# One tile pool for the up and down products, and five scan chunks moved from the output projection into the second half of the input projection

## The chip, the cores and the metric

The kernel runs on one core of one Trainium2 chip. The core has five engines that run their own instruction streams and meet through semaphores: TensorE (PE, matrix products into PSUM), VectorE (DVE), ScalarE (ACT), GpSimd (POOL) and SyncE (SP), whose queue (SPq) issues all DMAs of this kernel. The metric is the time of one execution on the device, in microseconds. Three runs of the kernel before took 2654.14, 2654.44 and 2649.2 us, a median of 2654.14.

## The reference

One layer of a sequence model on x of 2048 frames by 1024 channels, all in float32:

```python
h = rmsnorm(x, norm_mix_w)
u_b, u_c, u_h, z, xbc, dt_raw = split(h @ w_in)          # 3 x 1024, 1024, 1536, 16 columns
y_a = u_b * causal_conv3(u_c * u_h)                       # short convolution mixer
y_b = ssd_mixer(z, xbc, dt_raw, ...)                      # conv4 + SiLU on x/B/C, state scan, gate, grouped norm
x = x + concat(y_a, y_b) @ w_out
h = rmsnorm(x, norm_mlp_w)
x = x + square(relu(h @ w_up)) @ w_down                   # 1024 -> 4096 -> 1024
return rmsnorm(x, final_norm_w)
```

The mixer `ssd_mixer` has 16 heads in 2 groups. Its scan runs over chunks of the sequence: in a chunk, `y = (C B^T * decay) (x dt) + C state * exp(a)`, and then the state is decayed and gets the chunk's own `B^T (x dt decay_end)`. The reference writes chunks of 64 frames; the kernel takes 128 (`L`), which gives the same result, so there are 2 groups x 16 = 32 (group, chunk) units, in the list `CHUNKS` (line 1179), ordered by block of 512 frames, then group, then chunk. Units 0 to 15 belong to the first 1024 frames, 16 to 31 to the second.

## The kernel before

**Products.** Each float32 factor is split into a rounded part `hi` and a rest `lo` (ACT casts, line 100 or 205; DVE subtracts, line 101 or 206), and one product is three matmuls: hi hi, hi lo, lo hi. The large products (input projection, up, down) use a scheme of seven block products in place of eight: a 2 x 2 block product from sums and differences of blocks, in `Seven.chain` (line 245). Its seven products run in the order `b11, t1, t2, b21, t3, b22, t4`, each 12 matmuls of 128 x 128 by 128 x 512 when four pieces of the inner dimension are summed, so 84 for a *pair* of column tiles. After each product, `evict` takes a sum out of PSUM, `ahead` prepares weights of the next pair, and the callback `after(name)` interleaves other work.

**Stages,** in the order of time: the first half of the input projection (frames 0 to 1023), the second half (frames 1024 to 2047), the output projection in 64 units of 24 matmuls, up (two halves of 16 pairs), down with the final norm.

**The second half** (`second_half`, line 815) runs the 22 pairs of the list `LATER`; a name is the kind and the first tile: z (gate), x (inputs of the scan; x8 and x10 are B and C), ch (C and h of the short convolution), b. An x pair ends with two convolutions over 1024 frames (`conv`, line 679): one ACT pass, three DVE passes (line 685), a SiLU, a store to `xs_d`; one starts behind `b22`, one behind `t4`. Beside the pairs runs `side`, the generator `scan.run` (line 1330): `after` takes one step of it behind each of the seven products. It covers chunks 0 to 15.

**The scan.** With one set of buffers (`bufs` = 1, in the second half) a chunk takes 9 steps: `back` 1 (TensorE: `st`, `yo`, `yd`; DVE updates the state and adds), `back` 2 (adds D x from the tile `xd`, multiplies by the gate `y`) together with the loads of the next chunk (`bc`, `xd`, `dec`, `eb`), `back` 3 (squares), an empty step, `front` 1 of the next chunk (TensorE transposes x into `ptx` and B into `ptb`), `back` 4 (`pss`, the norm), `front` 2, `back` 5 (stores to `yn_d`) with the load of the next gate, `front` 3. In `front` (line 1245), step 2 has ACT do the decays (8 passes of line 1268, an exponential, line 1269), four multiplications by D (1271) and the cast `hi` of the weighted x (1276); step 3 has DVE subtract `lo` (1278) and multiply the decays by the masked scores (1279). `st` needs `hi` and `lo`, `yd` needs the decays. The tiles `xd`, `dec` and `y` have one buffer in the second half and two in the output projection, where a chunk takes 8 steps.

**The output projection.** A hook runs twice in each unit, behind 12 matmuls; in units 0 to 47 hook `at` takes `1 + at % 2` steps of the scan, for chunks 16 to 31. At hooks fixed by `schedule` (line 1498) blocks of y are fetched and split by ACT and DVE (`fill`, lines 1425 to 1427). From unit 48 on no scan runs.

**Up and down.** The pool `up` has eight tiles `utmp` of 512 columns, five `uhid` of 2 x 512 and two `facc`. A pair of up fills three `uhid` (e0, e1, e2), squares the relu on ACT, takes four differences on DVE (`sums`) and stores seven blocks to `hid_d` with four DMAs. When the stage ends, that pool closes and `down` (line 981) opens the pool `dp` in the same memory: 18 accumulators `acc`. `outs` (973) loads four of them for each d from x1; `evict` (line 1018) adds the sums of the down product into them. The steps of down (`STEPS`, line 1164) are: d = 0 with four inner tiles, d = 2 with two, then d = 1 with one and d = 3 with three together.

**Order on the engines.** A pool's slots go round: a new tile waits for the last reader of the tile that had its slot. The framework lays out each engine's instructions with some freedom: where one must wait, a later one that is ready may be placed ahead of it. On the chip each engine then keeps that order. Four PSUM banks take the sums of up and down (`x`, `y`), two more the sums `w`.

Of the kernel before, what the change touches and what calls it, by code (L numbers as in the profile page):

```python
# [39 lines left out]
def trunk(ctx: ExitStack, tc: tile.TileContext, x, w_in, w_dt, w_out, w_up, w_down, cvec, hrow, out):  # L40
# [150 lines left out]
    class Seven:  # L191
# [18 lines left out]

        def sums(self, e0, e1, e2, t4):

            self.sub(e2[:, 0], e2[:, 1], e0[:, 1])
            self.sub(e0[:, 1], e0[:, 1], e0[:, 0])
            self.sub(e1[:, 0], e2[:, 1], e0[:, 1])
            self.sub(t4, e1[:, 1], e1[:, 0])
# [210 lines left out]
    class Proj(Seven):  # L427
# [5 lines left out]
        LATER = "z0 x0 z4 ch0 ch1 b0 x8 ch2 ch3 b2 x2 ch4 ch5 b4 x4 x10 ch6 ch7 b6 x6 z6 z2".split()  # L433
# [381 lines left out]
        def second_half(self, ws, side):  # L815

            self.dt_weights()
            dts = itertools.chain(*(self.dt_part(NBB + bb) for bb in range(NBB)))
            for m, what in enumerate(self.LATER):
                last = m + 1 == len(self.LATER)  # L820
                ahead = self.plain(w_out[0], (0, 1)) if last else self.weights(1, self.LATER[m + 1])

                def after(name):
                    if m or name == "t4":
                        next(dts, None)
                    next(side, None)
                    if last:
                        proj_out.enter(self, name)

                ws = self.pair(1, what, ws, ahead, after)  # L830
            return ws

    class Mlp(Seven):
# [18 lines left out]
        def wide(self, name):  # L852
            return self.up.tile([P, 2, TB], F32, tag="uhid", name=name, bufs=5)

        def store(self, h, q, e0, e1, e2):
            t4 = self.tmp("t4")
            if h == 1 and q >= LAST:
                nc.sync.dma_start(b12_d[:, q - LAST], e0[:, 1])
            self.sums(e0, e1, e2, t4)
            for i, e in enumerate((e0, e1, e2)):  # L860
                nc.sync.dma_start(hid_d[h][q][:, 2 * i : 2 * i + 2], e)
            nc.sync.dma_start(hid_d[h][q][:, 6], t4)

        def pair(self, h, q, ws, ahead, after):

            e0, e1, e2 = (self.wide(n) for n in ("e0", "e1", "e2"))
            s = {}
# [5 lines left out]
            def add(o, pm, name):  # L873
                nc.vector.tensor_tensor(out=o, in0=pm, in1=s[name], op=ALU.add)
# [5 lines left out]
            def evict(name, gi, pm):  # L880
# [3 lines left out]
                elif name == "t1":  # L884
                    copy(pm["y"], "s5")
                elif name == "t2":
                    copy(pm["x"], "s2")
                elif name == "b21":
                    if gi in self.seeds:
                        relu2(e0[:, 0], pm["w"])  # L890
                    else:
                        add(e0[:, 0], pm["w"], "s1")
                        relu2(e0[:, 0], e0[:, 0])
                elif name == "t3":
                    add(e2[:, 1], pm["x"], "s5")
                    relu2(e2[:, 1], e2[:, 1])
                elif name == "b22":
                    add(e0[:, 1], pm["y"], "s2")
                    relu2(e0[:, 1], e0[:, 1])
                else:  # L900
                    relu2(e1[:, 1], pm["x"])

            got = self.chain([self.places], ws, ahead, evict, after)
            self.store(h, q, e0, e1, e2)
# [152 lines left out]
        def rest(self, ws):  # L1057
# [11 lines left out]
            sums = [self.dp.tile([P, TB], F32, tag="acc", name="facc", bufs=18) for _ in range(NBB)]  # L1069
# [34 lines left out]
        def norm_out(self, tiles, bb, ts, st, *sums):  # L1104
# [3 lines left out]
            r = st.spread()  # L1108
# [14 lines left out]
        def rstd(self, w=TB):  # L1123
            return Rstd(self.dp, lambda n: self.raw(n)[:, 0], D, w)

        def finish_first(self):

            for bb in range(NBB):
# [8 lines left out]
                acc = self.dp.tile([P, TB], F32, tag="facc", name="facc", bufs=1)  # L1137
# [41 lines left out]
    CHUNKS = [(b, g, c) for b in range(NB) for g in range(G) for c in range(NC)]  # L1179

    class Scan:
# [63 lines left out]
        def front(self, n):  # L1245
# [19 lines left out]

            dec = t["dec"]
            for i in range(HG):
                nc.scalar.activation(dec[:, i], dec[:, i], AF.Relu, bias=t["a"][:, i : i + 1], scale=-1.0)  # L1268
            nc.scalar.activation(dec, dec, AF.Exp, scale=-1.0)
            for j in range(4):  # L1270
                nc.scalar.mul(t["xd"][:, j], t["xd"][:, j], col(C_D, 4 * g + j))
            for k, by in (("xdt", "dt"), ("xde", "dend")):
                t[k] = self.tmp()
                nc.vector.tensor_tensor(out=byhead(t[k]), in0=byhead(xtok), in1=t[by], op=ALU.mult)
            hi, lo = t["parts"] = [a.bitcast(F32R) for a in (self.tile([512], "xtok", 1), self.tmp())]
            nc.scalar.copy(hi, t["xde"])
            yield
            nc.vector.tensor_tensor(out=lo, in0=t["xde"], in1=hi.bitcast(F32), op=ALU.subtract)
# [241 lines left out]
    with ExitStack() as c1:  # L1520
# [68 lines left out]
    mlp.down(c4, ws)  # L1589
# [57 lines left out]
```

## Time and profile before

| what | value |
|---|---|
| three runs | 2654.14, 2654.44, 2649.2 us; median 2654.14 |
| the profiled execution | 2651.32 us, of which the span of its instructions is 2649.1 us |
| mean granted TensorE clock | 0.995 |
| TensorE busy | 2597.8 us, 98% of the span |
| VectorE busy | 1926.7 us, 73% |
| ScalarE busy | 1455.0 us, 55% |
| DMA | 536.96 MB, 203 GB/s over the span |

The busy time of TensorE counts a matmul from its start to the end of its pipeline, 390 ns for one of 512 columns, though the next starts 227 ns later; so idle time counts, and not the share of busy time. A table of windows gives busy time by engine in a stretch of time; a list of waits names the engine that waited, what it waited for, the sum, how often, and the longest; a timeline has one row for each instruction, or for a run of like ones, with its start, its length, and in brackets the idle time ahead of it and what ended that.

### The profile page before, as it was taken

The numbers are of one execution on the slowest core, as the hardware profiler recorded it, in microseconds if no ns is written. First come the engines' busy times: TensorE is split into PE (matmuls) and PEld (weight loads), VectorE is DVE, ScalarE is ACT, GpSimd is POOL, SyncE is SP. The second block draws the span as 40 slices with busy tenths as digits, with TensorE's granted clock in tenths as the row PEclk, the third lists the DMA queues.
The fourth block names the chain that finished last, engine by engine and source line by source line (L and its number), as shares of the span: only waits on it lengthen the run. The fifth ranks groups of instructions, "written<-read, shape, count | busy, mean of one in ns | idle before, by whom it ended". The sixth has DMA issues, their size and how long they took to land.

```text
span 2649.1 us, 33645 instructions
## 1 busy us (share of the span) xinstructions
PE 2597.8 (98%) x12056; PEld 2133.7 (81%) x12056; DVE 1926.7 (73%) x2652; ACT 1455.0 (55%) x2212; POOL 54.0 (2%) x98
## 2 busy tenths in 40 slices
PE   7999999999999999999999999999999999999998
PEld 5788888788878888877888888888887888888887
DVE  7977867777778767767677775744447877888885
ACT  6654345776667666857336555755555444444543
POOL 0010000000000000000000000000000000000001
PEclk9999999999999999999999999999999999999999
DMA  3545745555555588877656786765558544665762
GB/s 145 197 175 187 274 143 200 185 161 171 175 163 165 163 272 258 265 205 220 202 203 230 258 314 238 273 216 192 197 194 290 155 151 150 217 205 176 244 207 69
DMA packets 292871, 536.96 MB, mean 203 GB/s; under 512 B 26208, under 2 KB 141920, under 8 KB 292704
## 3 DMA queue, kind: packets, MB, share of 16 engines
q1 hardware_dynamic: 292704, 534.82, 61.4%
q8 instruction: 94, 1.54, 0.2%
q14 instruction: 73, 0.60, 0.1%
HBM read 354.89 MB, written 179.83 MB: 202 GB/s over the span
## 4 chain that ended last, share of the span: by engine, by line
PE 61%; issue 25%; DMA 6%; ACT 5%; DVE 2%; SPq 0%; POOL 0%; POOLq 0%; DVEq 0%; ACTq 0%
PE px L276 9%; PE px L277 9%; PE px L278 9%; PE py L276 4%; PE py L278 4%; PE py L277 4%; PE pm L113 3%; PE pm L114 3%; PE pm L115 3%; DMA dec<-rd_d 3%; PE pw L276 2%; PE pw L278 2%; PE pw L277 2%; ACT dec L1268 1%; PE yd L1296 1%
## 5 line engine op out<-in xcount | busy, mean ns | idle before, releaser
L276 PE MATMUL px<-uh,whi 128*128 128x512 f32 x1672 | 656.5, 393 | 6.2 <-DVE acc L1018 2.0
L278 PE MATMUL px<-uh,wlo 128*128 128x512 f32 x1672 | 651.9, 390 | 0.0
L277 PE MATMUL px<-ul,whi 128*128 128x512 f32 x1672 | 651.5, 390 | 0.0
L276 PEld LDWEIGHTS px<-uh,whi 128*128 128x128 f32 x1672 | 314.2, 188 | 79.8 <-ACT s L727 3.6
L101 DVE TENSOR_TENSOR wlo<-wraw,whi 128x1024 fp32r<-128x1024 f32 x214 | 222.7, 1040 | 206.8 <-ACT whi L100 206.8
L278 PEld LDWEIGHTS px<-uh,wlo 128*128 128x128 f32 x1672 | 314.2, 188 | 66.2 <-issue 0.2
L277 PEld LDWEIGHTS px<-ul,whi 128*128 128x128 f32 x1672 | 314.4, 188 | 64.2
L100 ACT CAST whi<-wraw 128x1024 fp32r<-128x1024 f32 x214 | 193.9, 906 | 307.8 <-PE px L277 216.1
L100 ACT CAST whi<-s 128x1024 fp32r<-128x1024 f32 x210 | 219.8, 1047 | 227.8 <-PE py L277 98.1
L276 PE MATMUL py<-uh,whi 128*128 128x512 f32 x836 | 327.8, 392 | 5.4 <-DVE acc L1018 4.3
L277 PE MATMUL py<-ul,whi 128*128 128x512 f32 x836 | 325.9, 390 | 0.0
L278 PE MATMUL py<-uh,wlo 128*128 128x512 f32 x836 | 325.7, 390 | 0.0
L101 DVE TENSOR_TENSOR wlo<-s,whi 128x1024 fp32r<-128x1024 f32 x210 | 255.3, 1216 | 75.8 <-ACT whi L100 74.2
L113 PE MATMUL pm<-uh,whi 128*128 128x512 f32 (+1 forms) x648 | 251.7, 390 | 2.1 <-ACT uh L205 2.1
L114 PE MATMUL pm<-ul,whi 128*128 128x512 f32 (+1 forms) x648 | 248.6, 384 | 0.0
L115 PE MATMUL pm<-uh,wlo 128*128 128x512 f32 (+1 forms) x648 | 248.4, 383 | 0.0
L276 PEld LDWEIGHTS py<-uh,whi 128*128 128x128 f32 x836 | 157.2, 188 | 40.5 <-DVE acc L1018 4.8
L278 PEld LDWEIGHTS py<-uh,wlo 128*128 128x128 f32 x836 | 157.1, 188 | 32.9 <-DVE wlo L101 0.2
L277 PEld LDWEIGHTS py<-ul,whi 128*128 128x128 f32 x836 | 157.1, 188 | 32.0
L347 ACT CAST uh<-rh 128x1024 fp32r<-128x1024 f32 (+1 forms) x128 | 120.4, 944 | 80.7 <-PE py L278 62.7
L276 PE MATMUL pw<-uh,whi 128*128 128x512 f32 x418 | 163.3, 391 | 0.7 <-ACT pw L283 0.7
L278 PE MATMUL pw<-uh,wlo 128*128 128x512 f32 x418 | 162.9, 390 | 0.0
(239 smaller groups left out, 3777.1 us busy)
## 6 DMA issues: line engine op xcount, KB each, us to landing
hid_d<-e SPq DMA_DIRECT2D x96, 512.0 KB, 3.9
rh<-hid_d SPq DMA_DIRECT2D x96, 512.0 KB, 4.2
wraw<-w_in SPq DMA_DIRECT2D x68, 512.0 KB, 4.0
wraw<-w_down SPq DMA_DIRECT2D x104, 256.0 KB, 3.6
wraw<-w_up SPq DMA_DIRECT2D x48, 512.0 KB, 4.3
dec<-rd_d SPq DMA_DIRECT2D x32, 512.0 KB, 5.7
wraw<-w_out SPq DMA_DIRECT2D x32, 512.0 KB, 4.9
x_d<-xt SPq DMA_DIRECT2D x64, 256.0 KB, 3.5
```

The lines of the kernel that those rows point to most:

```text
L100: nc.scalar.copy(hi, raw)
L101: eng.tensor_tensor(out=lo, in0=raw, in1=hi.bitcast(F32), op=ALU.subtract)
L113: nc.tensor.matmul(out, whi, hi, start=(k == 0), stop=False)
L114: nc.tensor.matmul(out, whi, lo, start=False, stop=False)
L115: nc.tensor.matmul(out, wlo, hi, start=False, stop=(k == nk - 1))
L276: nc.tensor.matmul(p, hi, h[0], start=not seeded and k == 0, stop=False, **kw)
L277: nc.tensor.matmul(p, hi, h[1], start=False, stop=False, **kw)
L278: nc.tensor.matmul(p, lo, h[0], start=False, stop=(k == len(g) - 1), **kw)
L347: nc.scalar.copy(p[i][0], t)
L1268: nc.scalar.activation(dec[:, i], dec[:, i], AF.Relu, bias=t["a"][:, i : i + 1], scale=-1.0)
L1296: nc.tensor.matmul(yd[(i % 2) * 64 : (i % 2) * 64 + 64, (i // 2) * L : (i // 2 + 1) * L], byhead(t["xdt"])[:, i, :], t["dec"][:, i, :], st ...
```

## The change

Three edits go together.

1. **One pool.** The down product no longer opens a pool of its own. All tiles of 512 columns, the temporaries and blocks of a pair of up as well as the accumulators of down, come from one tag `acc` with 18 buffers in the pool `up`, which stays open to the end. A pair of up takes nine of them, each block in a tile of its own, and stores its seven blocks with seven DMAs of 256 KB. The accumulators are loaded in the order d = 0, 2, 1, 3. The tiles `facc` and the last norm's multiplier come from the same pool's tag `facc` (two buffers).
2. **Chunks.** The second half runs chunks 0 to 20 (`HERE = 21`) and takes two steps of the scan behind `t1` and `t3`, so 9 for each pair; chunks 21 to 31 remain for the output projection, whose hooks take one step, and two at every eighth. `LATER` is put in an order in which the tiles that chunks 16 to 20 need are made by the 16th pair.
3. **Order in `front`.** Step 2 now first weights x (`xde`, `xdt`) and casts `hi`, then does the decays, then `lo`; the multiplications by D move to step 3.

```diff
-        LATER = "z0 x0 z4 ch0 ch1 b0 x8 ch2 ch3 b2 x2 ch4 ch5 b4 x4 x10 ch6 ch7 b6 x6 z6 z2".split()
+        LATER = "z0 x0 z4 x8 x2 ch0 ch1 b0 x4 x10 ch2 ch3 b2 x6 z6 z2 ch4 ch5 b4 ch6 ch7 b6".split()
...
-                    next(side, None)
+                    for _ in range(1 + (name in ("t1", "t3"))):
+                        next(side, None)
...
         def tmp(self, name):
-            return self.up.tile([P, TB], F32, tag="utmp", name=name, bufs=8)
...
+            return self.up.tile([P, TB], F32, tag="acc", name=name, bufs=18)
+
+        BLOCKS = ("b11", "t1", "t2", "b21", "t3", "b22", "t4")
+
+        def store(self, h, q, e):
             if h == 1 and q >= LAST:
-                nc.sync.dma_start(b12_d[:, q - LAST], e0[:, 1])
...
+                nc.sync.dma_start(b12_d[:, q - LAST], e["t1"])
+            for n in ("t2", "t3", "t4"):
+                e[n] = self.tmp(n)
+            self.sub(e["t3"], e["b22"], e["t1"])
+            self.sub(e["t1"], e["t1"], e["b11"])
+            self.sub(e["t2"], e["b22"], e["t1"])
+            self.sub(e["t4"], e["b21"], e["t2"])
+            for i, n in enumerate(self.BLOCKS):
+                nc.sync.dma_start(hid_d[h][q][:, i], e[n])
...
-                t[n] = self.dp.tile([P, TB], F32, tag="acc", name="acc", bufs=18)
+                t[n] = self.tmp("acc")
...
-        def down(self, stack, ws):
-            self.dp = stack.enter_context(tc.tile_pool(name="dp", bufs=1, reuse_waits="tile"))
+        def down(self, ws):
             self.acc = {}
-            for d in range(4):
+            for d in (0, 2, 1, 3):
                 self.outs(0, d)
...
-            r = st.spread()
+            r = st.spread(self.facc()[:, 0 : st.w])
...
+    HERE = 21
...
+            for k, by in (("xde", "dend"), ("xdt", "dt")):
+                t[k] = self.tmp()
+                nc.vector.tensor_tensor(out=byhead(t[k]), in0=byhead(xtok), in1=t[by], op=ALU.mult)
+            hi, lo = t["parts"] = [a.bitcast(F32R) for a in (self.tile([512], "xtok", 1), self.tmp())]
+            nc.scalar.copy(hi, t["xde"])
             dec = t["dec"]
             for i in range(HG):
                 nc.scalar.activation(dec[:, i], dec[:, i], AF.Relu, bias=t["a"][:, i : i + 1], scale=-1.0)
             nc.scalar.activation(dec, dec, AF.Exp, scale=-1.0)
+            nc.vector.tensor_tensor(out=lo, in0=t["xde"], in1=hi.bitcast(F32), op=ALU.subtract)
+            yield
             for j in range(4):
                 nc.scalar.mul(t["xd"][:, j], t["xd"][:, j], col(C_D, 4 * g + j))
-            for k, by in (("xdt", "dt"), ("xde", "dend")):
...
-            side = scan.run(0, len(CHUNKS) // 2)
+            side = scan.run(0, HERE)
...
-            side = scan.run(len(CHUNKS) // 2, len(CHUNKS))
+            side = scan.run(HERE, len(CHUNKS))
...
-                for _ in range(1 + at % 2):
+                for _ in range(1 + (at % 8 == 0)):
                     next(side, None)
...
         ws = mlp.half(1, ws, iter(()))
-    mlp.down(c4, ws)
+        mlp.down(ws)
```

More of the change, by code (lines that the diff above doesn't have):

```diff
@@ L873, in add @@
             def add(o, pm, name):
-                nc.vector.tensor_tensor(out=o, in0=pm, in1=s[name], op=ALU.add)
+                e[o] = self.tmp(o)
+                nc.vector.tensor_tensor(out=e[o], in0=pm, in1=s[name], op=ALU.add)
+                relu2(e[o], e[o])
             def relu2(o, i):
@@ L1068, in rest @@
                     tiles[d + i, bb] = self.acc[1, d][n]
-            sums = [self.dp.tile([P, TB], F32, tag="acc", name="facc", bufs=18) for _ in range(NBB)]
+            sums = [self.tmp("facc") for _ in range(NBB)]
             for bb, t0, w in ((0, 0, TB), (1, 0, TB // 2), (1, TB // 2, TB // 2)):
@@ L1135, in load @@
                     return t
-                acc = self.dp.tile([P, TB], F32, tag="facc", name="facc", bufs=1)
+                acc = self.facc()
                 for d in range(0, KD, 2):
```

46 lines of the change are left out of this document (11 added, 35 removed).

## The prediction

> **What bounds the kernel now.** I read the busy line of the page first, then the table of windows by stage. A row there gives the window and its length, then the busy time of TensorE (PE), its weight loads, VectorE (DVE) and ScalarE (ACT), then clock and DMA share.
>
> ```profile
> PE 2597.8 (98%) x12056; PEld 2133.7 (81%) x12056; DVE 1926.7 (73%) x2652; ACT 1455.0 (55%) x2212; POOL 54.0 (2%) x98
> ...
> 470.00:975.00 505.00, 500.93 (x2500) 407.56 (x2499) 379.23 (x546) 344.77 (x582) 14.21 (x38) 1.00 0.57 176
> ...
> 975.00:1270.00 295.00, 285.27 (x1529) 233.78 (x1528) 218.72 (x354) 206.06 (x411) 0.00 (x0) 0.99 0.81 239
> ...
> 1420.00:1980.00 560.00, 560.00 (x2471) 463.28 (x2470) 318.84 (x399) 312.18 (x462) 0.00 (x0) 1.00 0.67 237
> ...
> 1990.00:2030.00 40.00, 34.29 (x139) 26.99 (x138) 30.41 (x40) 22.84 (x33) 0.00 (x0) 0.92 0.90 307
> 2030.00:2080.00 50.00, 48.78 (x214) 40.02 (x214) 43.88 (x59) 19.71 (x23) 0.00 (x0) 1.00 0.61 197
> ```
>
> TensorE sets the time in every stage, and the change takes no matmul away. So all it can win or lose is TensorE idle time and clock. The second half of the input projection (470 to 975) idles 505.00 - 500.93 = 4.1 us, the output projection with the scan beside it (975 to 1270) 9.7, the up product none in 560, and the seam between up and down (1990 to 2080) 5.7 + 1.2 = 6.9. Next I read TensorE's waits in three windows: the output projection, the second half, the seam.
>
> ```profile
> PE st L113 <- ACT xtok L1276: 8.1, 3, 4.5
> PE st L114 <- DVE stmp L1278: 1.1, 3, 0.6
> ...
> PE px L276 <- ACT s L727: 1.5, 2, 1.2
> PE ptx L1253 <- DMA xd<-xs_d: 1.2, 2, 0.8
> ...
> PE py L276 <- DVE acc L1018: 4.3, 1, 4.3
> PE px L276 <- DVE acc L1018: 1.2, 1, 1.2
> ```
>
> The longest two, 4.5 and 4.3 us, have a second price. In the two windows of 7 us behind them the clock column, third from the end, is far below 1:
>
> ```profile
> 1227.00:1234.00 7.00, 7.00 (x38) 5.88 (x37) 5.33 (x8) 3.03 (x6) 0.00 (x0) 0.67 0.50 156
> ...
> 2023.00:2030.00 7.00, 4.69 (x11) 3.73 (x12) 1.47 (x3) 0.00 (x0) 0.00 (x0) 0.54 0.99 333
> ```
>
> That is (1 - 0.67) x 7 = 2.3 and (1 - 0.54) x 7 = 3.2 us of clock lost there, some of it just before or while idle; I price each drop at 3 us. The most that can be won is thus about 9.6 + 3 in the output projection, 5.5 + 3 at the seam and 3 in the second half: 24 us.
>
> **The seam: one pool.**
>
> ```profile
> 2016.22 0.32 SPq L862 DMA_DIRECT2D hid_d<-t  x1
> ...
> 2019.05 6.53 SPq L978 DMA_DIRECT2D acc<-x_d  x11
> ...
> 2020.58 0.39 PE L278 MATMUL px<-uh,wlo 128*128 128x512 f32 x1
> 2025.31 0.79 PE L276 MATMUL py<-uh,whi 128*128 128x512 f32 x1 [4.34 <-DVE acc L1018]
> ...
> 2022.43 0.69 DVE L1018 TENSOR_TENSOR acc<-pw,acc 128x512 f32<-128x512 f32 x1 [0.79 <-DMA acc<-x_d]
> ```
>
> The down product adds into accumulators that are first loaded from x1. Not one load is issued before up's last store (2016.22), because the pool `dp` lies where `up` lay. The first add runs at 2022.43, and TensorE, its banks full of unread sums, stands from 2020.97 to 2025.31. In the new pool a pair of up takes 9 of 18 slots (s5, s2, b11, b22, t1, b21, t2, t3, t4), so the first 9 accumulators get the slots of the pair before the last, stored some 20 us earlier. That covers d = 0 and d = 2, which the first two steps need; hence the order 0, 2, 1, 3. The other 7 wait for the last pair, but serve the third step, which comes 4 x 7 x 3 + 2 x 7 x 3 = 126 matmuls later, 28.6 us at the pitch of 0.227 us between the starts of such matmuls. So both waits and the drop should go: 8.5 us. Against it: DVE is busy 30.4 of 40 us and then 43.9 of 50, and the adds now fall into the stretch in which it makes the `ul` halves of the refill. What it idles there (9.6 us) is as much as the time to be saved, so some short waits come back. I take 7 of 8.5, bounds 2 and 9.
>
> The stores of up become 7 of 256 KB for 3 of 512 and 1 of 256: 3 x 32 = 96 more issues at some 0.33 us (the row L862), 1 us of the queue in each 19 us pair. TensorE does not wait once in this stage, at a DMA share of 0.67; cost nothing, bound 5 us if the stores came too late for a slot to be written again two pairs on.
>
> ```profile
> hid_d<-e SPq DMA_DIRECT2D x96, 512.0 KB, 3.9
> ...
> hid_d<-t SPq DMA_DIRECT2D x32, 256.0 KB, 4.6
> ```
>
> A small store lands no sooner than a large one, so the queue of DMAs does get longer. The Trainium skill, DMA: Bandwidth & Descriptors, section Bandwidth, asks for batches of 1 MiB or more and so speaks against this edit; its table has 64 KB at 32% of peak and 1 MB at 78%. By an estimate from that table the stores would cost up to half as much again, the DMA share would go to some 0.75, and TensorE would still be busy throughout.
>
> Adds, squares and subtractions of a pair keep their number and length; the tail's multiplier goes to a tile with two buffers in place of one: nothing.
>
> **The output projection: 11 chunks in place of 16.** The price of one chunk comes from windows that hold all 32 of them (DVE third, ACT fourth), for the tiles stmp, dec, srstd and xd in turn, and two rows of table loads:
>
> ```profile
> 470.00:1280.00 810.00, 51.12 (x544) 34.84 (x544) 173.42 (x288) 39.60 (x64) 1.00 0.66 199
> ...
> 470.00:1280.00 810.00, 37.60 (x512) 28.75 (x512) 39.02 (x32) 116.31 (x288) 1.00 0.66 199
> ...
> 470.00:1280.00 810.00, 50.63 (x62) 11.41 (x31) 1.00 0.66 199
> ...
> 470.00:1280.00 810.00, 19.59 (x128) 15.41 (x128) 21.78 (x32) 43.13 (x128) 1.00 0.66 199
> ...
> L1323 ACT ACT_TABLE_LOAD x30 | 38.5, 1283 | 0.6
> ...
> L1269 ACT ACT_TABLE_LOAD x29 | 37.2, 1283 | 0.5
> ```
>
> DVE: (173.4 + 39.0 + 50.6) / 32 = 8.2, two updates of the state at 0.69 and two small ones, about 10.1 us. ACT: (39.6 + 116.3 + 11.4 + 43.1 + 75.7) / 32 = 8.9 and two small copies, about 9.8 us. Five chunks less take some 50 us off each engine here. The longest wait in detail:
>
> ```profile
> 1225.61 0.79 PE L113 MATMUL st<-xtok,btok 128*128 128x512 f32 x1 [4.47 <-ACT xtok L1276]
> ...
> 1224.00 1.06 ACT L1269 ACTIVATE dec<-dec 128x1024 f32<-128x1024 f32 x1
> 1224.96 0.60 ACT L1276 CAST xtok<-stmp 128x512 fp32r<-128x512 f32 x1
> ...
> 1222.16 1.22 DVE L1279 TENSOR_TENSOR dec<-dec,smask 128x1024 f32<-128x1024 f32 x1
> ...
> ACT dec L1268 <- DMA dec<-rd_d: 32.4, 10, 8.8
> ```
>
> DVE multiplies this chunk's decays at 1222.16, so the exponential at 1224.00 already belongs to the next chunk: ACT's order has the next chunk's decays, for which it waits 3 us on average, ahead of this chunk's cast. Moving the cast ahead of its own chunk's decays therefore doesn't remove this by itself. The lower rate does more: from the transposes to `st` are 5 steps; at 1.5 steps a hook that is 3.3 hooks of 2.72 us, 9 us, and at 1.125 it is 4.4, 12 us. With 3 us more lead the wait of 4.5 shrinks to 1.5, the others (at most 2.7) go, and the clock isn't lost. Of 9.2 + 3 I take 9, bounds 3 and 12; the fills of the next blocks of y stay bunched on ACT.
>
> **The second half: 21 chunks.** TensorE gains here what it loses there. Its chunk costs 3.9 us: two groups yd lie 28.4 apart (below) over 9 products of 12 x 0.227. A pair is then 84 x 0.227 + 3.9 = 23.0 us and holds exactly one chunk, where 9 steps to 7 made it 0.78. For a pair of x DVE has 10.1 for the chunk, 6 x 1.24 for the convolution, 4 splits and two sums:
>
> ```profile
> L685 DVE SCALAR_TENSOR_TENSOR cacc<-buf,cv,cacc 128x1024 f32<-128x1024 f32 x72 | 89.6, 1279 | 0.6 <-ACT cacc L683 0.3
> ...
> 470.00:975.00 505.00, 389.40 (x1243) 229.23 (x1241) 96.90 (x89) 83.22 (x89) 1.00 0.57 176
> ```
>
> 96.9 / 89 = 1.09 a split: 10.1 + 7.5 + 4.4 + 1.4 = 23.4 us in 23.0, or 102%; before it was 21.1 in 22.1, 95%. x8 x2 and x4 x10 now stand side by side, where before only x4 x10 did. The overload of 0.4 alone is 2.4 us over six pairs; the waits of this stage at 95% were 2.7. I take +5, and bounds of 0 and 35 (next part). Other pairs have 3 us and more to spare. Chunk 16 needs z2, one pair ahead of it; only DVE's multiplication by the gate would wait for that, with no matmul right behind it.
>
> **Sum:** -7 - 9 + 5 = -11. The profiled run took 2651.3 (a span of 2649.1 and 2.2 around it); the three runs gave 2649.2 to 2654.4 with a median of 2654.1, so it is 2.8 below the median and inside their spread. That gives 2640 from the one and 2643 from the other; since medians will be compared, I say **2643**.
>
> **Rivals.**
>
> ```profile
> 691.13 1.09 PE L1296 MATMUL yd<-dec,stmp 128*64 128x128 f32 x16
> ...
> 694.48 0.37 SPq L1220 DMA_DIRECT2D xd<-xs_d  x1
> ...
> 719.50 1.09 PE L1296 MATMUL yd<-dec,stmp 128*64 128x128 f32 x16
> ...
> 730.38 0.56 SPq L1220 DMA_DIRECT2D xd<-xs_d  x1
> ...
> xd<-xs_d SPq DMA_DIRECT2D x14, 256.0 KB, 4.3
> ```
>
> *Slower: the single `xd` buffer.* In the second half `xd` is loaded again only when DVE has added the old one, and the transposes, next on TensorE, need it. The load is issued 694.48 - 692.22 = 2.3 us after yd where DVE is free, 730.38 - 720.59 = 9.8 where a convolution lies ahead. From yd to the transposes there were 4 products, 10.9 us; with two steps behind t3 there are 3, 8.2. With 4.3 us to land it decides at 3.9 us of lag. At 9.8 TensorE waits 5.9 in a pair; in six pairs 35, so 2651 - 16 + 35 = 2670. For it: no margin beyond 1.6 us. Against it: all pairs now have the same phase, with yd behind b21, while the convolutions start behind b22 and t4, so DVE is at the chunk when it counts. 0.15.
>
> *No change: the waits move.* DVE is full at the seam and ACT in the fills; half of each saving returns, the second half eats the rest: -8 + 8, 2651 to 2655. 0.21.
>
> *All of it, at no cost:* -20, 2631 to 2634. 0.07.
>
> *The clock by another rule.* The Trainium skill, TensorE: Matmul & The Clock Gate, Part 1, has activity counted in free-running windows of 3.4 us, so a gap of 4.4 would hold a whole one only in some runs; here two of two such gaps were followed by a drop, and the gap of 2.7 by none. Were the drops chance, the runs before would hold them in part only, and the gain were -11 + 4 = -7: 2647. 0.05, still faster.
>
> *Forecast,* 2636 to 2648: 0.52.
>
> Faster by over 0.2% (5 us, about what a measurement here can tell from none): 0.52 + 0.07 + 0.05 less a bit at the edge, 0.62; same 0.22; slower 0.16. The range, 2630 to 2660, leaves out most of the slow rival and a little below.
>
> **What would show it.** Seam: `acc` loads issued well before up's last store, no wait on L1018 over 1 us, clock 1.00. Output projection: waits of `st` under 2 us, 20 us shorter for the chunks gone. Second half: 20 us longer for 5 chunks, plus the loss; if `ptx` waits for `xd`, or px for ACT and DVE in x pairs, by over 15 us in all, I was wrong.

## The result and the profile after

The changed kernel takes 2669.86 us, the median of four runs (2669.36 to 2676.79), beside 2651.67 us for four runs of the kernel before (2648.63 to 2654.44): a ratio on record of 1.0081, 95% interval 1.0065 to 1.0097 (the quotient of these two medians is 1.0069; the text goes by the ratios and intervals on record throughout). It is slower by 0.8%. The forecast was 2643 us, so it had the wrong sign, and 2670 lies outside its range.

The profiled execution of the changed kernel took 2676.79 us, 7 us more than its other runs, with a span of 2674.9. Its times by stage therefore show where the loss lies, and the ratios how large it is. The table of windows below is cut at the first matmul of the scan's `yo` in the second half, at the first of the output projection, at the first of up, and at the first add into an accumulator. First the kernel before, then the changed one; a row has the window, its length, and the busy time of TensorE (PE), weight loads, VectorE (DVE), ScalarE (ACT) and POOL, then clock, DMA share and GB/s.

```profile
476.40:962.30 485.90, 482.24 (x2418) 392.74 (x2419) 367.74 (x530) 336.94 (x571) 14.21 (x38) 1.00 0.56 171
962.30:1391.80 429.50, 419.77 (x2123) 344.82 (x2121) 312.74 (x477) 251.05 (x471) 0.00 (x0) 0.99 0.76 232
1391.80:2022.40 630.60, 627.01 (x2760) 517.21 (x2759) 377.90 (x476) 359.77 (x529) 0.00 (x0) 1.00 0.68 239
```

```profile
477.00:1009.70 532.70, 508.59 (x2599) 407.92 (x2598) 408.55 (x608) 379.13 (x669) 23.11 (x38) 1.00 0.57 173
1009.70:1411.30 401.60, 396.05 (x1943) 327.64 (x1942) 270.95 (x399) 204.72 (x371) 0.00 (x0) 1.00 0.73 227
1411.30:2047.60 636.30, 627.21 (x2737) 517.38 (x2737) 379.94 (x474) 358.37 (x526) 0.00 (x0) 0.99 0.69 236
```

| stage | length before | after | difference | TensorE idle before | after |
|---|---|---|---|---|---|
| second half | 485.9 | 532.7 | +46.8 | 3.7 | 24.1 |
| output projection | 429.5 | 401.6 | -27.9 | 9.7 | 5.6 |
| up and seam | 630.6 | 636.3 | +5.7 | 3.6 | 9.1 |

Length less idle time is 26.4 us more in the second half and 23.7 less in the output projection: what the five chunks cost, together with clock drops and with stands too short to count as idle. The difference that hurts is the idle time of the second half, 20.4 us more. VectorE is busy 77% of that stage (408.55 of 532.70) and ScalarE 71%: neither is full. What TensorE waited for there, by the list of waits of the changed kernel (sum, times, longest):

```profile
PE pss L1315 <- ACT xtok L1252: 9.9, 12, 1.6
PE ptx L1247 <- DMA xd<-xs_d: 6.6, 6, 1.8
PE py L269 <- ACT eb L758: 3.6, 1, 3.6
PE st L113 <- ACT xtok L1264: 1.9, 3, 1.3
```

The same list before had `pss` for `xtok` 0.6 us once and `ptx` for `xd` 1.2 us twice. Two new waits carry most of the loss, 16.5 of the 24.1 us; the 3.6 us of `py` for `eb`, a single stand at 847.0, were not followed up. One chunk of the changed kernel shows the first; these are rows of its timeline (start, length, engine or queue), TensorE's, ScalarE's and the two loads:

```profile
932.86 1.09 PE L1290 MATMUL yd<-dec,stmp 128*64 128x128 f32 x16
933.99 0.37 SPq L1216 DMA_DIRECT2D dec<-rd_d  x1
...
939.93 0.99 ACT L1267 ACTIVATE dec<-dec,dd 128x128 f32<-128x128 f32 x3 [7.71 <-DMA dec<-rd_d]
...
942.19 0.60 PE L1247 MATMUL ptx<-ident,xd 128*128 128x128 f32 x4
942.87 0.98 ACT L1267 ACTIVATE dec<-dec,dd 128x128 f32<-128x128 f32 x3
943.87 1.28 ACT L1268 ACT_TABLE_LOAD   x1
945.16 1.06 ACT L1268 ACTIVATE dec<-dec 128x1024 f32<-128x1024 f32 x1
...
946.63 0.58 ACT L1252 COPY xtok<-ptx 128x512 f32<-128x512 f32 x1
...
947.26 0.49 PE L1315 MATMUL pss<-ssq,ones_r 128*128 128x128 f32 x2 [1.41 <-ACT xtok L1252]
```

`dec` is a single buffer, free when `yd` ends (933.95), and loaded at once. ScalarE stands 7.71 us for it, though other work lies behind: VectorE ended `y` at 938.23, and ScalarE squares it only at 940.82, so its order is fixed. Then it does the whole decay block (eight passes, a table load, an exponential, 5.0 us, and 6.3 with what lies between) and only then copies `ptx` to `xtok`, 3.8 us after the transposes ended. `pss` wants the PSUM bank of `ptx`, so TensorE stands 1.41 us. A chunk of the kernel before with the same order:

```profile
894.44 1.09 PE L1296 MATMUL yd<-dec,stmp 128*64 128x128 f32 x16
...
904.06 1.06 ACT L1269 ACTIVATE dec<-dec 128x1024 f32<-128x1024 f32 x1
...
906.49 0.60 PE L1253 MATMUL ptx<-ident,xd 128*128 128x128 f32 x4
...
907.18 0.59 ACT L1258 COPY xtok<-ptx 128x512 f32<-128x512 f32 x1
```

The exponential comes ahead of the copy here too, but `ptx` ends 11.6 us after `yd`, not 8.8, and the block is over. Counted over the chunks of both timelines, the exponential lies ahead of the copy in 12 of 15 chunks before and in 13 of 20 after; the median from the end of `yd` to the end of `ptx` is 11.6 us before and 9.1 after; and from the end of `ptx` to the start of the copy it is 1.0 us on average before and 2.75 after.

The second new wait is the loop through `xd`. VectorE's last read frees the tile, the load goes out, and the transposes wait for it:

```profile
736.89 0.66 PE L1290 MATMUL yd<-dec,stmp 128*64 128x128 f32 x8
741.07 0.68 DVE L1305 TENSOR_TENSOR stmp<-stmp,xd 128x512 f32<-128x512 f32 x1
741.78 0.39 SPq L1214 DMA_DIRECT2D xd<-xs_d  x1
...
746.80 0.66 PE L1247 MATMUL ptx<-ident,xd 128*128 128x128 f32 x4 [0.64 <-DMA xd<-xs_d]
```

In the output projection the waits of `st` are gone; two others have come, and the up stage and the seam have four of 2 us or more. First the list of the output projection, then of up and of the seam, all of the changed kernel:

```profile
PE ptb L1249 <- DVE state L1300: 2.9, 2, 2.0
PE yo L1287 <- DMA bc<-xs_d: 2.7, 1, 2.7
...
PE px L269 <- ACT pw L276: 2.6, 1, 2.6
PE px L269 <- ACT s L866: 2.0, 1, 2.0
...
PE px L269 <- ACT pw L276: 3.5, 1, 3.5
PE px L269 <- DVE acc L1010: 2.0, 1, 2.0
```

Windows of 7 us behind two of them (the 2.6 of up and the 3.5 of the seam) show the clock below 1, third column from the end:

```profile
1724.00:1731.00 7.00, 4.45 (x15) 3.27 (x14) 5.81 (x8) 4.87 (x9) 0.00 (x0) 0.76 0.94 291
2038.00:2045.00 7.00, 5.88 (x14) 4.64 (x15) 4.36 (x8) 2.92 (x5) 0.00 (x0) 0.51 0.84 279
```

And the seam's loads of accumulators still come after up's last stores but one:

```profile
2040.76 1.52 SPq L858 DMA_DIRECT2D hid_d<-t  x2
2042.33 0.59 SPq L971 DMA_DIRECT2D acc<-x_d  x1
2043.17 0.32 SPq L858 DMA_DIRECT2D hid_d<-t  x1
2043.54 6.59 SPq L971 DMA_DIRECT2D acc<-x_d  x10
```

### The profile page after: what moved, and what is told of

It reads as the page before. It is cut to its first block, busy times and chain, and to the rows that moved or that the text cites. A ratio compares the mean times of both kernels' runs of the same rounds, so it can differ in the third digit from the quotient of the medians.

```text
span 2674.9 us, 33761 instructions
## 1 busy us (share of the span) xinstructions
PE 2603.6 (97%) x12056; PEld 2133.6 (80%) x12056; DVE 1929.1 (72%) x2652; ACT 1451.0 (54%) x2211; POOL 63.9 (2%) x98
## 4 chain that ended last, share of the span: by engine, by line
PE 75%; DMA 8%; ACT 6%; DVE 6%; issue 3%; SPq 1%; POOL 0%; POOLq 0%; ACTq 0%; DVEq 0%
PE px L269 11%; PE px L270 11%; PE px L271 11%; PE py L270 6%; PE py L269 5%; PE py L271 5%; PE pm L113 5%; PE pm L114 4%; PE pm L115 4%; PE pw L269 3%; PE pw L270 3%; PE pw L271 3%; DMA dec<-rd_d 2%; ACT dec L1267 1%; ACT whi L100 1%
```

## The experiments

Each ratio is the kernel's runs to those of the kernel before on the same chip, with its 95% interval.

| run | what it is | median us | ratio to before |
|---|---|---|---|
| after | the changed kernel | 2669.86 | 1.0081 [1.0065, 1.0097] |
| e1_pool | before + one pool | 2654.34 | 1.0023 [1.0014, 1.0032] |
| e2_chunks | before + 21 chunks, steps, order of pairs | 2671.06 | 1.0085 [1.0072, 1.0098] |
| e3_front | before + order in `front` | 2647.41 | 0.9996 [0.9986, 1.0005] |
| e4_order | before + order of pairs alone | 2662.57 | 1.0049 [1.0035, 1.0062] |
| e5_pssbank | after, `pss` in the bank of `yo` | 2673.09 | 1.0072 [1.0058, 1.0087] |
| e6_steps | after, double steps elsewhere | 2675.21 | 1.0093 [1.0077, 1.0109] |
| e7_spread | after, x pairs spread | 2672.31 | 1.0075 [1.0060, 1.0090] |
| e8_all | e2 + e3 + the edits of e5, e6, e7 | 2673.79 | 1.0080 [1.0065, 1.0095] |
| f2_decload | after, `dec` loaded later | 2667.17 | 1.0066 [1.0053, 1.0079] |
| f3_all | two pools, edits of e5, e7, f2 | 2661.14 | 1.0040 [1.0025, 1.0054] |
| f4_seam | e1, first accumulators loaded early | 2659.57 | 1.0027 [1.0015, 1.0040] |
| f5_18 | before + 18 chunks + front | 2662.98 | 1.0052 [1.0039, 1.0065] |
| g1_xd2 | after, two buffers of `xd` | 2665.07 | 1.0058 [1.0045, 1.0070] |
| g2_xd2dec | after, f2 and g1 together | 2652.42 | 1.0007 [0.9998, 1.0017] |
| g3_all | f3 + two buffers of `xd` | 2647.18 | 0.9993 [0.9983, 1.0003] |
| g4_18 | g3 with 18 chunks | 2646.18 | 0.9985 [0.9976, 0.9994] |
| g5_16 | g3 with 16 chunks | 2659.42 | 1.0023 [1.0012, 1.0035] |
| g6_2pools | g2 with two pools | 2651.90 | 0.9996 [0.9985, 1.0008] |

### First: the three edits one by one

Four theories of the second half: **W**, the places of the doubled steps; **R**, five more chunks are too much for ScalarE and VectorE; **F**, the new order in `front`; **P**, the order of the pairs.

`e1_pool`: the edit of the pool as in the diff above, nothing else.

> The kernel before with the one pool alone (the up product writes seven single blocks, the accumulators come from its slots); chunks, steps, order of the pairs and the scan's front as before. My forecast's step said: the accumulators' loads go out early, the seam gains 7 us, so 2645. Its rival, read from the trace after: the slots are handed out in the order of the program, the last pair's t2, t3 and t4 come before the accumulators, so the loads still go out after the last store (seam 0), while TensorE waits in up for px released by ScalarE where it did not before (+3 to +8 us), so 2651 to 2660. All theories of the second half: no change there, its time without TensorE stays near 4 us.

1.0023: the rival's range. The loads go out no earlier (the first at 2018.27, behind a row of two stores that starts at 2016.52 and ahead of the last one at 2018.93), and in up px waits 2.1 us for ScalarE's `pw` at the change of halves, with the clock at 0.76 in the 7 us around.

`e2_chunks`: the edits of chunks, steps, `LATER` and hook, nothing else.

> The kernel before with 21 chunks in the second half (new order of pairs, two steps after t1 and t3, other hook in the output projection), pools and the scan's front as before. Theory W (the loss comes from the places of the doubled steps: pss falls one product after ptx whose PSUM bank it takes, ptx two products after its xd load): the second half loses 15 to 20 us, output projection gains 6, so 2660 to 2666, with waits of pss for xtok and ptx for xd in the trace. Theory R (five more chunks overfill VectorE and ScalarE): the same time, but waits of yd or st for VectorE and ScalarE spread over the x pairs. Theory F (the new order in the scan's front makes ScalarE late): no loss in the second half, 2644 to 2648.

1.0085: the whole loss. F falls. At 2671 us the time is above the 2660 to 2666 that W, and R with it, gave. The waits are those of after: `ptx` for `xd` 7.1 us in 7 places, `pss` for `xtok` 6.8 in 9.

`e3_front`: the edit of `front` alone.

> The kernel before with the new order in the scan's front alone (decay factors in the second step, behind the cast of xde). Theory F: pss and ptx wait as after, 10 us or more lost, 2660 or more. Theories W, R and P (order of the pairs): 0, within 3 us of the kernel before, 2649 to 2655.

0.9996, no difference. The output projection keeps its wait of `st` (7.8 us in 2 places), and e2, with the lower rate and the old order in `front`, has none there; so what took it away in the changed kernel is not the earlier cast.

`e4_order`:

```diff
-        LATER = "z0 x0 z4 ch0 ch1 b0 x8 ch2 ch3 b2 x2 ch4 ch5 b4 x4 x10 ch6 ch7 b6 x6 z6 z2".split()
+        LATER = "z0 x0 z4 x8 x2 ch0 ch1 b0 x4 x10 ch2 ch3 b2 x6 z6 z2 ch4 ch5 b4 ch6 ch7 b6".split()
```

> The kernel before with the new order of the 22 pairs of the second half alone, 16 chunks, one step after each product. Theory P (x, B, C and z pairs side by side load ScalarE and VectorE so that the scan is late): 10 us or more lost among those pairs, 2660 or more. Theories W, R and F: 0, 2649 to 2655.

1.0049, as P said, with 16 chunks still. Its list of waits in the second half:

```profile
PE px L276 <- ACT s L727: 4.9, 6, 2.0
PE pss L1321 <- ACT xtok L1258: 3.8, 5, 2.3
```

Both are ScalarE late, in the x pairs and in the pairs just behind them. So P alone would be over half of the loss, if it added to the rest.

### Second: one edit each on the changed kernel

`e5_pssbank`:

```diff
-            pss = psum("tp", "pss", 2) if self.bufs == 1 else psum("mw", "pss")
+            pss = psum("k4", "pss") if self.bufs == 1 else psum("mw", "pss")
```

> The changed kernel with one edit: in the second half pss takes the PSUM bank of yo, which is read and free by then, instead of the bank that ptx has just filled and that ScalarE's xtok copy must empty first. Theory B (that bank is the wait: 9.9 us in the trace after): pss no longer waits for xtok, 6 to 10 us less than after, 2657 to 2664. Theory R (ScalarE is late anyway, the bank only shows it): the wait comes back at the next product that needs ScalarE (srstd, dec or px), within 3 us of after, 2664 to 2672.

1.0072, an interval that holds the changed kernel's 1.0081: the 6 to 10 us of theory B are not there. The wait moves on, to `st` and to more of `ptx`:

```profile
PE ptx L1247 <- DMA xd<-xs_d: 7.8, 9, 1.8
PE st L113 <- ACT xtok L1264: 4.8, 5, 1.7
```

`e6_steps`:

```diff
-                    for _ in range(1 + (name in ("t1", "t3"))):
+                    for _ in range(1 + (name in ("b11", "t1"))):
```

> The changed kernel with one edit: the two doubled steps of each pair come after b11 and t1, not t1 and t3, so that three products instead of two lie between xd's load and ptx, and the steps that free and load xd stand alone. Theory W (ptx waits for xd, 6.6 us in the trace after, since load and ptx are two products apart): that wait goes to under 1.5 us and 5 to 9 us come off, 2659 to 2665. Theories B, P and R: the pss waits stay or grow, within 3 us of after, 2664 to 2672.

1.0093. The waits for `xd` fall to 3.9 us, not under 1.5, and `pss` keeps 9.8: W is at most a part. The transposes `ptx` end 11.6 us after `yd` in the median here, as late as in the kernel before, and the copy still starts 2.2 us behind them; so what makes the copy late is not that distance alone.

`e7_spread`: `LATER` as in the text below.

> The changed kernel with one edit: the order of the 22 pairs, z0 x0 z2 x8 ch0 ch1 b0 x2 ch2 ch3 b2 x10 z4 ch4 ch5 b4 x4 z6 x6 ch6 ch7 b6, so that the x pairs are spread and still come before the chunks that need them. The order alone cost the kernel before 0.49%, 13 us. Theory P (x pairs side by side): 8 to 13 us come off, 2655 to 2662. Theories W, B and R: under 3 us, 2664 to 2672.

1.0075: P falls at 21 chunks, though it was shown at 16. `pss` still waits 10.9 us. The same 20 us cannot be lost twice: what the order costs is covered here by a wait that stands there anyway.

`e8_all`: the three edits together, with two pools.

> The kernel before with 21 chunks in the second half and the new front of the scan, its two pools kept (the one pool alone cost 0.23%), and with pss in yo's bank, the doubled steps after b11 and t1, and the spread order of the pairs. If theories B, W and P hold together, the second half loses under 5 us, the output projection keeps its gain of 6, the seam is as before: 2643 to 2650, faster than both kernels or level with the one before. If theory R holds (five more chunks are too much for ScalarE and VectorE wherever they stand), over 2658.

1.0080, and `st` now waits 8.0 us for `xtok`. R is all that is left of the theories, and it names no mechanism. So I read ScalarE's rows again, and found the decay block ahead of the `xtok` copy, as shown in the section on the result.

### Third: the decay block, the seam, and the number of chunks

`f2_decload`:

```diff
-            t["dec"] = self.tile([HG, L], "dec")
-            nc.sync.dma_start(t["dec"], rd_d[b][r0 : r0 + HG, 0, :].partition_broadcast(P))
+            if self.bufs == 2 or n == self.begin:
+                self.load_dec(n)
...
                     next(back)
                     yield
+                    self.load_dec(n + 1)
                     yield
                     next(front, None)
```

> The changed kernel with one edit: in the second half dec is loaded two steps later, with the empty step ahead of ptx, and not right after yd. Theory D: ScalarE takes the decay block (8 relu, a table load, an exp, some 5 us) 5 to 6 us after yd, when dec has landed; at 9 steps a pair ptx comes 9 us after yd, where before it came 14 us after, so the block falls on the xtok copy (2.5 us late on average after, 0.9 before) and pss, st and the projection's px wait behind it. With the later load the block comes behind the xtok copy: that lag goes under 1.2 us, the pss waits under 3 us, 6 to 12 us come off, 2657 to 2663, unless yd now waits for dec, which it would show. Theory R (every engine queue is simply too full at 9 steps a pair): within 3 us of after, 2666 to 2673, the waits move to another product.

1.0066, 2667 us: by its time this is R's range and not D's, and the interval doesn't tell it from the changed kernel. But the waits do what D said and one thing more:

```profile
PE ptx L1254 <- DMA xd<-xs_d: 13.7, 14, 2.1
PE pss L1322 <- ACT xtok L1259: 3.2, 6, 0.7
```

`pss` for `xtok` falls from 9.9 to 3.2, and `ptx` for `xd` doubles. The load itself leaves only 0.6 us after `yd` in the median (the layout lifts it); what has changed is ScalarE's order: the exponential lies ahead of the copy in 6 of 20 chunks, not 13. (The 14 us of the expectation are one chunk, the median before is 11.6; its 2.5 and 0.9 us are 2.75 and 1.0 counted with care.)

`f3_all`: the edits of e5, e7 and f2 together, two pools.

> The kernel before with 21 chunks in the second half, the new front and its two pools kept, with dec loaded in the empty step, pss in yo's bank, and the spread order of the pairs. Theory D with B and P: the second half loses under 8 us and the output projection keeps its 6: 2645 to 2653. Theory R: over 2660, as every mix of 21 chunks so far.

1.0040, 2661 us: half of the loss is gone, and still the time is R's (over 2660) and not D's. 8.3 us of `ptx` for `xd` remain.

`f4_seam`:

```diff
                         self.refill((0, 1, 2, 3), name)
+                        if name == "t2":
+                            self.acc = {}
+                            self.outs(0, 0)
+                            self.outs(0, 2)
...
-            self.acc = {}
-            for d in (0, 2, 1, 3):
+            for d in (1, 3):
```

> The kernel before with the one pool, and the loads of the first eight accumulators put out during the last pair of up (their tiles taken ahead of t2, t3 and t4 of that pair). The one pool alone was 1.0023 of before and its accumulators still loaded after the last store. The step of my forecast (early loads take the accumulators' waits, 3.9 us in that trace, and the clock drop behind them away: 7 us): 0.9995 to 1.0000 of before, no wait of px for acc over 1 us. Rival (TensorE waits there for pw and ScalarE anyway, 3.2 us, and the drop stays): 1.0015 to 1.0030.

1.0027. The loads do go out early, and px's longest wait for `acc` is 0.8. But no time is won; TensorE waits once, for ScalarE. That cast waits for VectorE's sums of weights, and these for a load of `w_down` that is issued at 2031.42, behind the other eight accumulator loads (from 2026.85 on), and lands at 2037.50. The load row of the timeline, and the list of waits at the seam:

```profile
2000.66 5.73 SPq L974 DMA_DIRECT2D acc<-x_d  x8
...
PE py L269 <- ACT whi L100: 4.7, 1, 4.7
PE px L269 <- DVE acc L1012: 0.8, 1, 0.8
```

`f5_18`: `HERE = 18`, one doubled step in a pair, 14 chunks in the output projection.

> The kernel before with 18 chunks in the second half instead of 16 (8 steps a pair, one doubled after t1; the old order of the pairs with z2 and z4 exchanged), 14 in the output projection, and the new front; two pools. Theory R and theory D alike (a chunk each 8 products falls between 9 and 7): the second half loses 4 to 10 us more than before, output gains 2 to 3, 1.001 to 1.003 of before. If the loss begins only where ptx falls within 9 us of yd at every chunk: no loss, 0.998 to 0.9995.

1.0052, with `ptx` for `xd` 8.2 us and `pss` for `xtok` 5.3: two more chunks without more buffers already lose most of it.

### Fourth: the two loops together

`g1_xd2`:

```diff
-            t["xd"] = self.tile([4, L], "xd")
-            nc.sync.dma_start(t["xd"], xs_d[h][:, 4 * g : 4 * g + 4, ts])
+            if self.bufs == 2 or n == self.begin:
+                self.load_xd(n)
...
                     front = self.front(n + 1) if n + 1 < end else iter(())
+                    self.load_xd(n + 1)
                     next(back)
```

with `load_xd` taking `self.tile([4, L], "xd", 2)`.

> The changed kernel with one edit: in the second half xd has two buffers and the next chunk's xd is loaded one step earlier, so its load no longer waits for VectorE's last read of the chunk before. Theory X (the single xd buffer closes a loop yd, VectorE's add of xd, load, ptx): ptx waits for xd fall from 6.6 to under 1 us. If X alone is the cause, 12 us or more come off, under 2658; if X and D share it, 4 to 7 us, 2661 to 2666, and the pss waits for xtok stay near 10; if R holds, the waits move to pss, st and px, 2667 to 2673.

1.0058: what the expectation gave for X and D sharing it, though the interval still touches the changed kernel's. There is no wait for `xd` left, and `pss` stays:

```profile
PE pss L1322 <- ACT xtok L1259: 11.7, 12, 2.2
```

`g2_xd2dec`: the edits of f2 and g1.

> The changed kernel with both edits, dec loaded in the empty step and xd in two buffers. If X and D share the loss: ptx for xd under 1 us, pss for xtok under 4, the second half loses under 8 us, 2652 to 2658. If R holds: 2663 or more, with the loss at st, yd, yo or the projection's px.

1.0007, at the low end of what X and D allow. Alone, the two edits take 0.15 and 0.23 points off 1.0081, neither of them clear of the noise; together 0.74, or some 20 us. TensorE's idle time in the second half says the same: 24.1 us in the changed kernel, 22.7 in f2, 19.3 in g1, 9.5 in g2. Each loop alone had been standing behind the other. The window of its second half, and the longest of its waits there:

```profile
479.00:993.50 514.50, 504.99 (x2599) 407.71 (x2599) 411.45 (x608) 375.98 (x667) 24.27 (x38) 1.00 0.58 179
```

```profile
PE pss L1329 <- DVE ssq L1326: 2.3, 2, 2.0
PE pss L1329 <- ACT xtok L1266: 2.2, 3, 1.6
```

It is 18.2 us shorter than in the changed kernel, with 9.5 us of idle time for 24.1, at the same VectorE work (411.45 for 408.55) and ScalarE work: R is out. The chunk of the timeline that answers to the one shown above now has the copy ahead:

```profile
940.91 1.09 PE L1304 MATMUL yd<-dec,stmp 128*64 128x128 f32 x16
...
950.25 0.60 PE L1261 MATMUL ptx<-ident,xd 128*128 128x128 f32 x4
...
952.02 0.57 ACT L1266 COPY xtok<-ptx 128x512 f32<-128x512 f32 x1
...
955.94 1.06 ACT L1282 ACTIVATE dec<-dec 128x1024 f32<-128x1024 f32 x1
```

Over the stage the exponential lies ahead of the copy in 2 of 20 chunks, and the copy starts 1.7 us behind `ptx` on average, not 2.75, though `ptx` still ends 8.8 us after `yd` in the median.

`g3_all`: f3 with two buffers of `xd`. `g4_18`: the same with 18 chunks.

> The kernel before with 21 chunks in the second half, the new front, its two pools, dec loaded in the empty step, pss in yo's bank, the spread order of the pairs, and xd in two buffers. It was 1.0040 of before with one xd buffer and 8.3 us of ptx waits for xd. X and D: those go, 0.998 to 1.001 of before. R: 1.003 or more.

> As the run before it in this list, with 18 chunks in the second half (8 steps a pair, the old order of the pairs with z2 and z4 exchanged) and 14 in the output projection. With one xd buffer and dec early 18 chunks were 1.0052 of before, with ptx waits for xd of 8.2 us and pss waits of 5.3. X and D: 0.997 to 1.000. R: 1.002 or more.

0.9993, level with the kernel before; and 0.9985 [0.9976, 0.9994], the fastest version found, 4 us below the kernel before on the same chip. That is at the edge of what can be measured. (f5, which the expectation of g4 compares with, had neither `dec` loaded early nor `pss` in the bank of `yo`, so three edits lie between f5 and g4.)

`g5_16`: g3's edits with 16 chunks. `g6_2pools`: g2 with two pools.

> The kernel before, 16 chunks and its own order of the pairs and steps, with the new front, dec loaded in the empty step, pss in yo's bank and xd in two buffers. If the gain of the 18 chunks comes from the chunks that left the output projection, this one keeps that stage's waits and drop (8 to 11 us) and is 0.999 to 1.001 of before; if it comes from the buffers, 0.997 to 0.999.

> The changed kernel with both mends (xd in two buffers, dec in the empty step), but with the two pools of before; order of the pairs, places of the steps and the bank of pss as changed. With the one pool it was 1.0007 of before, and the one pool alone cost the kernel before 0.23%: if these add up, 0.998 to 0.999; if the pool costs nothing here, 1.0005 to 1.0015.

With 16 chunks the edits win nothing (1.0023, slower than either expectation), so g4's gain is not that of the buffers alone. The reason is open: in the profiled execution of g5 the second half and the output projection together take 915.4 us, exactly as in the kernel before. g6 is at 0.9996 and g2 at 1.0007: the intervals overlap, and the price of the one pool is not settled there; on the kernel before it is 0.23%.

## Why the forecast was wrong, step by step

**What bounds the kernel:** right as a frame. TensorE sets the time in every stage, and the whole loss is its idle time and clock.

**The output projection, -9:** right in kind, too large. The waits of `st` went with the lower rate and not with the earlier cast, as e3 shows; new waits of 2.9 and 2.7 us took part of it back, so the idle time fell by 4.1 us, not by the 6 that the term put beside 3 of clock. That the stage is 27.9 us shorter where the forecast had 28.5 is partly luck: apart from idle time it lost 23.7 us with the five chunks, not 19.5.

**The second half, +5: the step that failed.** It should have become 24.5 us longer, with the chunks, and became 46.8. Of the 22.3 us between, 15.4 are the idle time, 20.4 for 5. The other 6.9 (26.4 for 19.5) are a slower clock, 1.7 us, and stands too short to count as idle; they are not the price of a chunk, for in g3 five more chunks take 501.7 - 482.2 = 19.5 us, as forecast. The +5 was worked out from VectorE's sum in an x pair, 102% of the pair. But a sum by engine says nothing of when each piece comes, and the waits do not keep to the x pairs: four of the twelve stands of `pss`, 3.9 of 9.9 us, come after 890 us, when the last convolution has been over since 830. What decided was ScalarE, to which the term gave no price at all: a decay block that starts when `dec` has landed, some 5.5 us after its load, stands ahead of the copy that TensorE's next products need; at 9 steps a pair these products come 2.5 us sooner after `yd`. Beside it stands the loop through the single `xd` buffer, which the forecast kept as a rival. g2 shows the two together: with the copy ahead, and `xd` out of the way, the loss goes, at the same work. That the 2.5 us alone make the copy late is not shown; e6 speaks against it.

**The slower rival, the single `xd` buffer:** it named 2670 us, and 2670 it was, but by luck: its mechanism was half of the cause. It put 35 us into six x pairs; `ptx` waited 6.6 us for `xd` in all, never over 1.8. Its threshold holds: with `yd` ending at 737.55 and the load out at 741.78, 4.2 us later, TensorE waits 0.64 where the rival said from 3.9 on. Taking the buffer away as a cause (g1) brought back 0.23 points of 0.81, with an interval that barely tells it from nothing.

**The seam, -7:** failed. The step said that the first nine accumulators get the slots of the pair before the last, so that their loads go out early. But in the program the loads come behind the last pair's stores, on the same queue, and those wait for VectorE's differences `t2`, `t3` and `t4`, taken behind the last product; the slots of these three are handed out ahead of the accumulators' too, and which of the two orders held the loads was not separated. From 2000 to 2100 us TensorE idles 6.5 us where it idled 6.9. With the tiles taken and the loads put out ahead of those (f4) the loads left at 2000.66 and the wait for `acc` went, yet no time was won: the rival "the waits move" holds at the seam. There they moved to the next weights, behind the rest of the accumulator loads; a kernel with those weights loaded first was not tried.

**Up, nothing:** the seven stores cost TensorE nothing that I could see, but px now waits for ScalarE at the change of halves, 2.6 us in the changed kernel and 2.1 in e1, each with a clock drop; e1 puts the pool as a whole at 0.23%. Which of its parts makes `pw` late is open. The DMA share of up and seam went from 0.68 to 0.69, not to some 0.75 as the prediction estimated.

**The order of the pairs:** the forecast gave it no price of its own beside the six x pairs; at 16 chunks it costs 0.49% (e4). At 21 chunks its removal changed nothing that can be measured (e7).

## What to carry to other kernels

When more work is woven into a stage, do not ask only whether each engine has room: for each single buffer and each shared PSUM bank, write down the loop that frees it, loads it and needs it again, and hold its length against the new distance between those products. Look at what stands ahead of the needed piece in an in-order engine, above all a piece that waits for a DMA. And where two such loops are about as long, mending one shows little: 0.15 and 0.23 points alone were 0.74 together here.

## What the runs showed of the hardware

A clock drop followed gaps shorter than I had priced. TensorE stood 2.0 us from 1434.9 on in the changed kernel, and a drop followed; in the kernel before it stood 2.5 us from 1162.0 on, and none followed. (A stand of 2.7 us, as the prediction has it, is in no row of waits; the longest one without a drop is this one.) So the length of a gap alone doesn't decide. From 30 to 2600 us the traces' record of the clock has only two values, 1.00 and 0.50, and in every run its drops begin a whole number of steps of 3.413 us apart (in the changed kernel at 850.17, 1024.25, 1437.27, 1727.40 and 2038.01) and last one step or two. Cut along these steps, the 2.0 us lie within one step, and the next runs at half clock; the 2.5 us lie across a border. The first two rows are of the changed kernel, the other two of the kernel before; length less TensorE's busy time is the idle time in the step:

```profile
1433.86:1437.27 3.41, 1.44 (x7) 0.89 (x6) 3.35 (x7) 1.94 (x3) 0.00 (x0) 1.00 1.00 384
1437.27:1440.68 3.41, 3.41 (x10) 2.63 (x9) 0.56 (x1) 0.07 (x1) 0.00 (x0) 0.50 0.98 323
...
1159.94:1163.35 3.41, 2.05 (x10) 1.36 (x8) 3.05 (x7) 3.38 (x8) 0.00 (x0) 1.00 0.53 168
1163.35:1166.76 3.41, 2.01 (x11) 1.53 (x11) 2.26 (x3) 3.35 (x4) 0.00 (x0) 1.00 0.24 82
```

Over the 20 traces of this case, counted over the same stretch, each of the 56 steps at full clock in which TensorE idled 1.93 us or more was followed by a drop, none of the 315 in which it idled from 0.6 to under 1.72 us was, and of the 16 between them 5 were. A drop of one step costs 1.7 us and one of two steps 3.4: the two of the kernel before were of two, so the 3 us of the prediction fitted them, while four of the five above are of one.

The Trainium skill, TensorE: Matmul & The Clock Gate, Part 1, counts activity in free-running windows of 3.4 us; the steps of 3.4 us agree with that, and so does a gap that costs or not by where it falls. But these gaps are shorter than the idle window of about 3.4 us that it names, so the window need not be idle throughout. The prediction's rival on the clock had the windows right and went wrong where it wanted a whole one idle.
